# One pass of modulation products ahead of each group's keys, and opening transfers of two feature tiles

## The chip, the cores and the metric

The program runs on one core of a Trainium2 chip. The metric is the device time of one launch in microseconds (us), the median of several runs. The engines of the core are TensorE (PE: matmuls), VectorE (DVE), ScalarE (ACT), GpSimd (POOL) and SyncE (SP), whose part here is to issue transfers; 16 DMA engines move the data. Each engine works through its own queue in order and waits on semaphores.

## The reference, cut to what matters

Two layers of a diffusion backbone over 512 latent tokens and 256 context tokens of 1024 features. What the change touches is how layer 0 begins: a modulation vector is made from the conditioning vector, the inputs are scaled and shifted by it, and the modulated inputs are projected.

```python
silu_c, silu_cc = jax.nn.silu(c), jax.nn.silu(c_ctx)
mod = silu_c @ ada_w[layer] + ada_b[layer]              # 1024 x 6144
sh_m, sc_m, gt_m, sh_f, sc_f, gt_f = split(mod, 6)
u = x * (1 + sc_m) + sh_m                               # 512 x 1024
mod_c = silu_cc @ ada_w[layer][:, :2 * D] + ada_b[layer][:2 * D]
ctx_u = ctx * (1 + mod_c[D:]) + mod_c[:D]               # 256 x 1024
p = u @ w_in                # queries, keys, values, gates, pools, 16 scalars a token
pc = ctx_u @ (the columns of keys, values and scalars of w_in)
...                         # DeltaNet heads || pooling, o = [heads, pools]
y = o @ w_out
x = layernorm(ALPHA * x + gt_m * y)
...                         # ConvFFN, then layer 1
```

## The kernel before

Activations lie with features on the partitions: 8 tiles of 128 features by 512 tokens (latent) and 8 of 128 by 256 (context). An f32 product is made of three passes, high by high, low by high and high by low part: ACT copies the high part out of a tile (`ah`, `ch`, `w_hi`) and DVE or POOL subtracts it from the tile to get the low part (`al`, `cl`, `w_lo`). A projection's matmuls all stand in the helper `gemm` (L222).

The opening is `start` (from L241). The scale and shift columns that layer 0 needs first are 2048 columns of `ada_w`, in 4 groups g of 512: group g holds what the feature tiles 2g and 2g+1 need. One group goes through these steps:

- eight 128x512 f32 tiles `ada_w` (256 KB each) arrive by SP's queue; PE multiplies each by the two conditioning vectors `cs` (L289), the first four and the last four tiles into the same four strips of `ada_ps`;
- ACT copies the sums out as `ada_rows` (L304), PE turns them into columns `ada_t` with small matmuls (L311), and DVE adds the biases: `m` (L320);
- DVE scales and shifts the two tiles `x_in` (each as two halves of 256 tokens) and `c_in` (L325), ACT copies their high parts (L452), DVE and POOL make the low parts (L453);
- PE adds the two tiles' share of the 16 scalars, `scalars(g)` (L342, 8 matmuls into `scal_ps`), and of the first keys, `keys(2g)` and `keys(2g+1)` (L222, 12 matmuls each into `qkv_ps`), whose weights were split earlier.

The order on PE is written out by hand: products of the first four tiles of group g+1, `scalars(g)`, `keys(2g)`, products of the last four tiles of group g+1, `keys(2g+1)`, `ada_t` of group g+1. After the fourth group come `scalars(3)`, `keys(6)`, `keys(7)`, and then the small matmuls `sc_t` (L699), with which the opening ends for what follows here. Instructions that the code pins keep the order of the program; a scheduler places the others.

SP issues the transfers in the order of the program: per group eight `ada_w`, then for each of two feature tiles two halves of `x_in` and one `c_in`; behind the first and the second group two raw weight tiles, and at the end `even_k`, raw weights and `crow`. All these tiles borrow buffers of the pool "even" that later stages use under other names (`BUFS` gives their numbers, `tags` and `htags` the order in which they are borrowed).

One place far behind the opening matters too, the output projection of layer 0 (`out_proj`, in the trace from 330 to 400 us). There the residual tiles `z` are loaded by SP (L1321) into a new pool laid over memory of the closed pool "even", so that the loads wait for the last readers of what stood there; behind them in SP's queue come `ada_w` tiles of layer 1, which DVE multiplies by `crow` and sums (L358, the columns `mod` come from these sums, L367). On DVE the same queue holds the evictions `z<-out_ps` (L520) and some of the weight splits `w_lo` (L176).

## Time and profile before

| what | value |
|---|---|
| median of 3 runs | 1341.77 us (1341.52 to 1342.78) |
| the profiled execution, its own time | 1340.33 us |
| span of the profiled execution | 1338.5 us |
| mean granted clock of TensorE | 0.975 of full speed |
| PE busy | 1271.3 us (95%) |
| DVE, POOL, ACT busy | 907.3, 680.5, 583.9 us |
| bytes moved | 166.59 MB |

The profile is of one execution. Its own time is 1.83 us longer than its span and lies 1.44 us below the median. A matmul's busy time includes its overlap with the next one, so a stretch's length is read from starts, not from sums. Times in the rows below count from the span's start. SPq is SP's queue while it issues transfers; "idle before <- releaser" is how long the engine stood idle and what ended it.

### The profile page before, as it was taken

What the parts mean: (1) busy time and instruction counts of PE and PEld (TensorE: products, weight loads), DVE (VectorE), ACT (ScalarE), POOL (GpSimd) and SP (SyncE); (2) the same over time, 40 slices, a digit from 0 to 9 for tenths busy, and PEclk for the clock granted to TensorE, in tenths of its full rate; (3) what the DMA queues carried; (4) which work ended last, traced back from release to release, by engine and by line L of the source; (5) the groups of instructions that cost most, each with busy time, mean ns of one, the idle gap of its engine ahead of it and who ended that gap; (6) DMA issues with size and microseconds to landing.
All of it is one profiled execution on the core that took longest, in us unless ns stands there. A gap on an engine that the chain in (4) does not pass through costs nothing.

```text
span 1338.5 us, 19585 instructions
## 1 busy us (share of the span) xinstructions
PE 1271.3 (95%) x6690; PEld 1069.2 (80%) x6690; DVE 907.3 (68%) x1865; ACT 583.9 (44%) x1091; POOL 680.5 (51%) x616
## 2 busy tenths in 40 slices
PE   6898899989889999999999999999999999999997
PEld 2587777878688888888888988778988888888886
DVE  3397899999776787788644668956676666661125
ACT  2355414445547433333322576545463334332235
POOL 1336447666445665555444566966143433443453
PEclk8899999999988999999999999999899999999998
DMA  9521221522523555656566432323123323333344
GB/s 302 201 87 46 42 60 53 166 83 87 173 81 105 163 189 190 198 194 196 185 206 195 141 111 87 95 87 107 35 95 99 98 95 96 101 91 96 93 123 126
DMA packets 104948, 166.59 MB, mean 124 GB/s; under 512 B 20944, under 2 KB 29200, under 8 KB 104848
## 3 DMA queue, kind: packets, MB, share of 16 engines
q1 hardware_dynamic: 93888, 164.09, 39.2%
q10 hardware_dynamic: 10960, 1.25, 0.7%
q8 instruction: 53, 0.87, 0.3%
q14 instruction: 47, 0.39, 0.1%
HBM read 162.60 MB, written 2.69 MB: 123 GB/s over the span
## 4 chain that ended last, share of the span: by engine, by line
PE 73%; DVE 11%; POOL 4%; issue 3%; ACT 2%; DMA 2%; SPq 0%; ACTq 0%; POOLq 0%; DVEq 0%
PE prod_ps L222 37%; PE out_ps L222 22%; PE half_ps L222 3%; DVE ada_w L358 2%; POOL w_lo L176 1%; PE qkv_ps L222 1%; POOL conf_far L1221 1%; PE ln_e L413 1%; PE it_ps L987 1%; PE gate_ps L222 1%; PE dd_ps L862 1%; DVE x_t L933 1%; DMA ada_w<-in_ada 1%; POOL cb_t L886 1%; PE ln_w L423 1%
## 5 line engine op out<-in xcount | busy, mean ns | idle before, releaser
L176 POOL TENSOR_TENSOR w_lo<-w_raw,w_hi 128x512 fp32r<-128x512 f32 (+1 forms) x299 | 385.0, 1292 | 449.8 <-ACT w_hi L170 441.5
L170 ACT CAST w_hi<-w_raw 128x512 fp32r<-128x512 f32 (+1 forms) x408 | 246.2, 608 | 454.1 <-PE out_ps L222 149.8
L222 PE MATMUL prod_ps<-uh,w_lo 128*128 128x512 f32 x792 | 308.9, 390 | 2.6 <-POOL w_lo L176 2.6
L222 PE MATMUL prod_ps<-uh,w_hi 128*128 128x512 f32 x792 | 308.7, 390 | 0.6 <-ACT w_hi L170 0.6
L222 PE MATMUL prod_ps<-ul,w_hi 128*128 128x512 f32 x792 | 308.4, 389 | 0.0
L601 DVE SCALAR_TENSOR_TENSOR f_acc<-prod_ps,prm,f_acc 128x441 f32<-128x441 f32 (+2 forms) x320 | 222.4, 695 | 60.1 <-ACT f_acc L590 50.8
L176 DVE TENSOR_TENSOR w_lo<-w_raw,w_hi 128x512 fp32r<-128x512 f32 (+1 forms) x109 | 87.0, 799 | 137.7 <-ACT w_hi L170 135.1
L222 PEld LDWEIGHTS prod_ps<-uh,w_lo 128*128 128x128 f32 x792 | 148.7, 188 | 35.2 <-POOL w_lo L176 4.3
L222 PEld LDWEIGHTS prod_ps<-uh,w_hi 128*128 128x128 f32 x792 | 148.8, 188 | 31.9 <-ACT w_hi L170 1.5
L222 PEld LDWEIGHTS prod_ps<-ul,w_hi 128*128 128x128 f32 x792 | 148.7, 188 | 30.4
L222 PE MATMUL out_ps<-ah,w_lo 128*128 128x256 f32 (+1 forms) x352 | 119.6, 340 | 5.6 <-DVE w_lo L176 5.6
L222 PE MATMUL out_ps<-ah,w_hi 128*128 128x256 f32 (+1 forms) x352 | 120.0, 341 | 4.6 <-ACT w_hi L170 2.9
L222 PE MATMUL out_ps<-al,w_hi 128*128 128x256 f32 (+1 forms) x352 | 120.5, 342 | 0.0
L222 PE MATMUL out_ps<-hl,w_hi 128*128 128x512 f32 (+1 forms) x280 | 98.3, 351 | 0.0
L222 PE MATMUL out_ps<-hh,w_hi 128*128 128x512 f32 (+1 forms) x280 | 98.0, 350 | 0.0
L222 PE MATMUL out_ps<-hh,w_lo 128*128 128x512 f32 (+1 forms) x280 | 98.0, 350 | 0.0
L222 PEld LDWEIGHTS out_ps<-ah,w_lo 128*128 128x128 f32 x352 | 68.4, 194 | 12.8 <-DVE w_lo L176 5.9
L222 PEld LDWEIGHTS out_ps<-ah,w_hi 128*128 128x128 f32 x352 | 68.5, 195 | 12.2 <-ACT w_hi L170 3.4
L358 DVE SCALAR_TENSOR_TENSOR ada_w<-ada_w,crow_ps 128x512 f32<-128x512 f32 x112 | 70.8, 683 | 8.7 <-DMA ada_w<-in_ada 8.7
L222 PEld LDWEIGHTS out_ps<-al,w_hi 128*128 128x128 f32 x352 | 68.5, 195 | 7.7 <-DVE al L453 0.8
L222 PEld LDWEIGHTS out_ps<-hl,w_hi 128*128 128x128 f32 x280 | 52.7, 188 | 7.7
L222 PEld LDWEIGHTS out_ps<-hh,w_lo 128*128 128x128 f32 x280 | 52.6, 188 | 7.7
(362 smaller groups left out, 2323.4 us busy)
## 6 DMA issues: line engine op xcount, KB each, us to landing
ada_w<-in_ada SPq DMA_DIRECT2D x192, 256.0 KB, 4.0
w_raw<-in_ffn_up SPq DMA_DIRECT2D x176, 256.0 KB, 2.6
w_raw<-in_ffn_down SPq DMA_DIRECT2D x100, 256.0 KB, 2.7
w_raw<-in_even_in SPq DMA_DIRECT2D x40, 256.0 KB, 2.9
w_raw<-in_odd_in SPq DMA_DIRECT2D x40, 256.0 KB, 2.7
w_raw<-in_even_out SPq DMA_DIRECT2D x16, 256.0 KB, 2.8
w_raw<-in_odd_out SPq DMA_DIRECT2D x16, 256.0 KB, 2.8
w_raw<-in_ffn_down SPq DMA_DIRECT2D x20, 128.0 KB, 2.1
```

What stands on the lines that cost most here:

```text
L170: r = nc.scalar.copy(out=hi[:, :n], in_=raw)
L176: r = eng.tensor_tensor(out=lo[:, :n], in0=raw, in1=hi[:, :n].bitcast(F32), op=SUB)
L222: r = nc.tensor.matmul(out=o, lhsT=w, rhs=x[k][:, c0:c1], start=clear and k == i == 0, stop=k == n - 1 and i == 2, skip_group_check=pin)
L358: r = nc.vector.scalar_tensor_tensor(out=w, in0=w, scalar=1.0, in1=c, op0=MUL, op1=MUL, accum_out=self.mod[:, k, i:i + 1])
L413: nc.tensor.matmul(out=pe[:, 2 * (n * e + i):2 * (n * e + i) + 2], lhsT=t[:, i * P:(i + 1) * P], rhs=ones, start=e == 0 and i == 0 and not ...
L423: nc.tensor.matmul(out=o, lhsT=self.ones, rhs=d[:, 0:n].rearrange("p a b -> p (a b)"), start=True, stop=True)
L601: nc.vector.scalar_tensor_tensor(out=o, in0=sv[:, r0 + dr:r1 + dr, q0 + dc:q1 + dc], scalar=w[:, tap:tap + 1], in1=o, op0=MUL, op1=ADD)
L862: nc.tensor.matmul(out=o, lhsT=self.tri[:, 2 + d], rhs=r, start=d == 0, stop=d == 1)
L886: nc.gpsimd.tensor_tensor(out=t, in0=m[:, 2 * c:2 * c + 2], in1=self.mask(self.blk, 2), op=MUL)
L933: nc.vector.tensor_tensor(out=t, in0=a2[w, :, r, r + 1:16][:, :, None, :].broadcast_to([96, 2, m, m]), in1=x[w, :, r + 1:16, r + 1:16].rea ...
L987: nc.tensor.matmul(out=pt[:, h], lhsT=m[:, h], rhs=r1[:, h], start=True, stop=True)
L1221: nc.gpsimd.tensor_tensor(out=far, in0=far, in1=f, op=ADD)
```

## The change

In the opening the transfers are made larger: `ada_w` tiles come two at a time (128x1024, 512 KB), `x_in` comes as one 128x1024 transfer for the two feature tiles of a group and `c_in` as one of 128x512. They have buffers of their own in a pool "start", which is closed at the end of the opening: 12 of `ada_w`, 3 (`XB`) each of `x_in` and `c_in`. PE makes the products of all eight tiles of group g+1 in one go, then `scalars(g)`, then `ada_t` of group g+1, and only then `keys(2g)` and `keys(2g+1)`. One more weight, `even_in[6]`, is split at a pinned place in the fourth group; its raw tiles stand at the same place in SP's queue as before. The tiles of `big` and `t2` move to a pool "even2", which is opened when "start" is closed and lies over its memory; the tiles `ch` and `cl` borrow other buffers.

```diff
--- before.py
+++ after.py
@@ -83,10 +83,8 @@
 ODD = 'c0 c1 s0 c2 s1 c3 s2 s3'
 PK, RAWS, SPLITS = 4, 4, 4
 WK = [0, 1]
-EARLY = 1
+XB = 3
 KT = 1
-PIN_ADA = 0
-BIG = ("p0", "p1", "late", "tmp")
 BUFS = dict(p0=4, p1=4, late=4, tmp=5, kc=4, vc=2, vt=5, el=4, ec=2, mg=8, inv=10, z=3, at=2, n1=2, vn=2, kd=4, s0=2, s1=2,
             oo=8, osq=1, ada=4)
 
@@ -241,29 +239,32 @@
     def start(self, km):
 
         nc, a = self.nc, self.a
-        tags = [t for t in ("p0", "p1", "late", "ec", "el", "mg", "vt") for _ in range(self.bufs[t])]
-        htags = [t for t in ("kc", "vc", "n1", "at", "s0", "s1", "kd", "vn", "oo") for _ in range(self.bufs[t])]
+        with ExitStack() as ctx:
+            return self.start_in(km, self.pool("start", ctx=ctx))
+
+    def start_in(self, km, sp):
+        nc, a = self.nc, self.a
+        htags = [t for t in ("n1", "at", "s0", "s1", "kd", "vn", "oo") for _ in range(self.bufs[t])]
         half = lambda i, dt, nm: self.ep.tile([P, C], dt, tag=htags[i], bufs=self.bufs[htags[i]], name=nm)
         aw, xi, ci, wk = [], [], [], {}
+
         for g in range(4):
-            for k in range(KD):
-                t = tags.pop(0) if g < 3 or k < 4 else "ada"
-                w = (self.ada_tile(0) if t == "ada" else self.big("ada_w", t)[:, 0:T] if t in BIG else
-                     self.t2(t, "ada_w").rearrange("p a b -> p (a b)"))
-                nc.sync.dma_start(out=w, in_=a["ada0"][g, :, k])
-                aw.append(w)
-            for k in (2 * g, 2 * g + 1):
-                xi.append([self.ep.tile([P, C], F32, tag="inv", bufs=self.bufs["inv"], name="x_in") for _ in HALVES])
-                for x, (c0, c1) in zip(xi[k], HALVES):
-                    nc.sync.dma_start(out=x, in_=a["xT"][:, k, c0:c1])
-                ci.append(half(k, F32, "c_in"))
-                nc.sync.dma_start(out=ci[k], in_=a["ctxT"][:, k])
+            for k in range(0, KD, 2):
+                w = sp.tile([P, 2, T], F32, tag="aw", bufs=12, name="ada_w")
+                nc.sync.dma_start(out=w, in_=a["ada0"][g, :, k:k + 2])
+                aw += [w[:, 0], w[:, 1]]
+            x = sp.tile([P, 2, T], F32, tag="x", bufs=XB, name="x_in")
+            nc.sync.dma_start(out=x, in_=a["xT"][:, 2 * g:2 * g + 2])
+            xi += [[x[:, i, c0:c1] for c0, c1 in HALVES] for i in range(2)]
+            c = sp.tile([P, 2, C], F32, tag="c", bufs=XB, name="c_in")
+            nc.sync.dma_start(out=c, in_=a["ctxT"][:, 2 * g:2 * g + 2])
+            ci += [c[:, 0], c[:, 1]]
             if g in WK:
                 i = WK.index(g) * PK * P
                 wk[g] = [self.raw(a["even_in"][4 + m][:, i:i + PK * P]) for m in range(2)]
         nc.sync.dma_start(out=km, in_=a["even_k"])
-        self.ch = [half(8 + k, F32R, "ch") for k in range(KD)]
-        self.cl = [half(16 + k, F32R, "cl") for k in range(KD)]
+        self.ch = [half(k, F32R, "ch") for k in range(KD)]
+        self.cl = [half(8 + k, F32R, "cl") for k in range(KD)]
         cs = self.cp.tile([P, KD, 2], F32, name="cs")
         nc.scalar.activation(out=cs, in_=self.cvec, func=AF.Silu)
         raw, wsc = (self.ep.tile([P, C], dt, tag="z", bufs=self.bufs["z"], name=f"scal_{nm}") for nm, dt in
@@ -288,30 +289,31 @@
                 q = 32 * (k % 4)
                 r = nc.tensor.matmul(out=ps[q:q + 2, :], lhsT=cs[:, k, :], rhs=aw[8 * g + k],
                                      start=k < 4, stop=k >= 4, skip_group_check=True)
-                if PIN_ADA:
-                    self.tc.keep_in_program_order(r)
-
-        for g in range(4):
+                self.tc.keep_in_program_order(r)
+
+        def clear():
             ps = self.mm("ada_ps")
             nc.vector.memset(ps, 0.0)
-            ada(g, ps, range(4))
+            return ps
+
+
+        ps = clear()
+        for g in range(4):
+            ada(g, ps, range(KD))
+            rows = sp.tile([P, T], F32, tag="rows", bufs=2, name="ada_rows")
+            nc.scalar.copy(out=rows, in_=ps)
             if g:
                 self.scalars(psc, wsc, g - 1)
-                if EARLY:
-                    keys(2 * g - 2)
-            ada(g, ps, range(4, 8))
-            rows = self.big("ada_rows")[:, 0:T]
-            nc.scalar.copy(out=rows, in_=ps)
-            if g:
-                if not EARLY:
-                    keys(2 * g - 2)
-                keys(2 * g - 1)
             pt = self.gd("ada_t")
             for j in range(4):
                 r = nc.tensor.matmul(out=pt[:, 2 * j:2 * j + 2], lhsT=rows[:, j * P:(j + 1) * P], rhs=self.sel2,
                                      start=True, stop=True)
-                if PIN_ADA:
-                    self.tc.keep_in_program_order(r)
+                self.tc.keep_in_program_order(r)
+            if g < 3:
+                ps = clear()
+            else:
+
+                self.early = {6: [w for x in self.raws(a["even_in"][6]) for w in self.piece(x, pin=True)]}
 
             ptv = pt[:, 0:8].rearrange("p (s n w) -> p s n w", s=2, n=2)
             for s in range(2):
@@ -328,6 +330,9 @@
             if g in wk:
                 for m in range(2):
                     ws[m] += self.piece(wk[g][m], pin=True)
+            if g:
+                keys(2 * g - 2)
+                keys(2 * g - 1)
         self.scalars(psc, wsc, 3)
         keys(6)
         keys(7)
@@ -634,6 +639,7 @@
             self.ep = self.pool("even", ctx=ctx)
             self.ada_tile = lambda k: self.ep.tile([P, T], F32, tag="ada", bufs=self.bufs["ada"], name="ada_w")
             first, scal = self.start(km)
+            self.ep2 = self.pool("even2", ctx=ctx)
             self.dp = ctx.enter_context(self.tc.tile_pool(name="scratch", bufs=1, space=bass.MemoryType.DRAM))
             self.gate = [None] * H
             ps, pooled, self.decays = {}, [], {}
@@ -673,7 +679,7 @@
         self.dbg("mixl", self.al)
 
     def big(self, name, tag="tmp"):
-        return self.ep.tile([P, T + 16], F32, tag=tag, bufs=self.bufs[tag], name=name)
+        return self.ep2.tile([P, T + 16], F32, tag=tag, bufs=self.bufs[tag], name=name)
 
     def t1(self, tag, name=None):
 
@@ -681,7 +687,7 @@
 
     def t2(self, tag, name=None):
 
-        return self.ep.tile([P, 4, P], F32, tag=tag, bufs=self.bufs[tag], name=name or tag)
+        return self.ep2.tile([P, 4, P], F32, tag=tag, bufs=self.bufs[tag], name=name or tag)
 
     def gates(self, scal):
 
@@ -788,7 +794,7 @@
     def qkv(self, m, lat, con, pre=None):
 
         nc, ep = self.nc, self.ep
-        ws = pre or self.weights(self.a["even_in"][m])
+        ws = pre or self.early.pop(m, None) or self.weights(self.a["even_in"][m])
         w = self.gconv[:, m]
         for x, h, l, n in ((con, self.ch, self.cl, C), (lat, self.ah, self.al, T)):
             if x is None:
```

On PE, in the opening: `ada_ps` are the products, `ada_t` the columns' matmuls, `scal_ps` the scalars, `qkv_ps` the keys. Before, the last four products of group 1 stand between the two blocks of keys of group 0:

```order
L222 MATMUL qkv_ps<-cl,w_hi 128x256
L222 MATMUL qkv_ps<-ch,w_lo 128x256
L289 MATMUL ada_ps<-ada_w,cs 2x512 x4
L222 MATMUL qkv_ps<-ah_75,w_hi 128x512
L222 MATMUL qkv_ps<-al_83,w_hi 128x512
```

and the columns of that group stand behind both blocks (the first rows are the end of `keys(1)`):

```order
L222 MATMUL qkv_ps<-cl,w_hi 128x256
L222 MATMUL qkv_ps<-ch,w_lo 128x256
L311 MATMUL ada_t<-prm,ada_rows 128x2 x4
L289 MATMUL ada_ps<-ada_w,cs 2x512 x4
L342 MATMUL scal_ps<-ah_76,scal_w 32x512
L342 MATMUL scal_ps<-al_84,scal_w 32x512
L342 MATMUL scal_ps<-ch,scal_w 32x256
L342 MATMUL scal_ps<-cl,scal_w 32x256
L342 MATMUL scal_ps<-ah_77,scal_w 32x512
```

Now, from the columns of group 0 on:

```order
L309 MATMUL ada_t<-prm,ada_rows 128x2 x4
L290 MATMUL ada_ps<-ada_w,cs 2x512 x8
L347 MATMUL scal_ps<-ah_74,scal_w 32x512
L347 MATMUL scal_ps<-al_82,scal_w 32x512
L347 MATMUL scal_ps<-ch,scal_w 32x256
L347 MATMUL scal_ps<-cl,scal_w 32x256
L347 MATMUL scal_ps<-ah_75,scal_w 32x512
L347 MATMUL scal_ps<-al_83,scal_w 32x512
L347 MATMUL scal_ps<-ch,scal_w 32x256
L347 MATMUL scal_ps<-cl,scal_w 32x256
L309 MATMUL ada_t<-prm,ada_rows 128x2 x4
L220 MATMUL qkv_ps<-ah_74,w_hi 128x512
```

All eight products of group 1 stand ahead of the scalars of group 0, and the columns of group 1 ahead of the keys of group 0.

On SP, in the opening, one group's transfers before, with the start of the next group:

```order
L253 DMA ada_w<-in_ada 128x512 x8
L258 DMA x_in<-in_xT 128x256 x2
L260 DMA c_in<-in_ctxT 128x256
L258 DMA x_in<-in_xT 128x256 x2
L260 DMA c_in<-in_ctxT 128x256
L162 DMA w_raw<-in_even_in 128x512 x2
L253 DMA ada_w<-in_ada 128x512 x8
```

and now:

```order
L254 DMA ada_w<-in_ada 128x1024 x4
L257 DMA x_in<-in_xT 128x1024
L260 DMA c_in<-in_ctxT 128x512
L160 DMA w_raw<-in_even_in 128x512 x2
L254 DMA ada_w<-in_ada 128x1024 x4
```

The group's bytes and their place in the queue are the same; 14 transfers have become 6.

On SP, in the output projection, the eight loads of `z` and the first of `ada_w` with the semaphores that they wait for, before:

```order
L1321 DMA z_3535<-in_xT 128x512 [waits DMAHW5_49,DMAHW0_49,DMAHW6_49,DVE_49,DMAHW7_49,PE_49,Pool_49]
L1321 DMA z_3536<-in_xT 128x512
L1321 DMA z_3537<-in_xT 128x512
L1321 DMA z_3538<-in_xT 128x512
L1321 DMA z_3539<-in_xT 128x512 [waits DMAHW1_49]
L1321 DMA z_3540<-in_xT 128x512 [waits DMAHW2_49]
L1321 DMA z_3541<-in_xT 128x512 [waits DMAHW3_49]
L1321 DMA z_3542<-in_xT 128x512 [waits DMAHW4_49]
L356 DMA ada_w<-in_ada 128x512 [waits DMAHW5_49]
L356 DMA ada_w<-in_ada 128x512 [waits DMAHW6_49]
```

and now:

```order
L1327 DMA z_3479<-in_xT 128x512 [waits DMAHW5_49,DMAHW0_49,DMAHW6_49,DVE_49,DMAHW7_49,PE_49,Activation_49]
L1327 DMA z_3480<-in_xT 128x512
L1327 DMA z_3481<-in_xT 128x512
L1327 DMA z_3482<-in_xT 128x512
L1327 DMA z_3483<-in_xT 128x512 [waits DMAHW1_49]
L1327 DMA z_3484<-in_xT 128x512 [waits DMAHW2_49]
L1327 DMA z_3485<-in_xT 128x512 [waits DMAHW3_49]
L1327 DMA z_3486<-in_xT 128x512 [waits DMAHW4_49]
L361 DMA ada_w<-in_ada 128x512 [waits DMAHW5_49,DVE_49,Pool_49]
L361 DMA ada_w<-in_ada 128x512 [waits DMAHW6_49]
```

The `z` loads no longer wait for POOL; the first `ada_w` behind them now waits for DVE and POOL itself. DVE's value for `z` was that of its last `al<-gate` split, and is now that of `oo<-oo,oss`, six rows of DVE ahead of it.

On DVE, in the output projection, from that last split on, before:

```order
L453 TENSOR_TENSOR al_89<-gate,ah_81 128x512
L176 TENSOR_TENSOR w_lo<-w_raw,w_hi 128x512
L520 SCALAR_TENSOR_TENSOR z_3535<-out_ps,mod_g,z_3535 128x512
L520 SCALAR_TENSOR_TENSOR z_3536<-out_ps,mod_g,z_3536 128x512
L358 SCALAR_TENSOR_TENSOR ada_w,mod<-ada_w,crow 128x512 x4
L520 SCALAR_TENSOR_TENSOR z_3537<-out_ps,mod_g,z_3537 128x512
L358 SCALAR_TENSOR_TENSOR ada_w,mod<-ada_w,crow 128x512 x4
L367 TENSOR_TENSOR mod_3757<-mod 128x16
L368 TENSOR_TENSOR mod_3757<-mod_3757,prm 128x16
L377 SCALAR_TENSOR_TENSOR cols_f_3760<-mod_3757,prm 128x8
L378 SCALAR_TENSOR_TENSOR cols_f_3760<-mod_3757,prm 128x8
L379 TENSOR_TENSOR cols_f_3760<-cols_f_3760,mod_3757 128x8
```

and now:

```order
L458 TENSOR_TENSOR al_89<-gate,ah_81 128x512
L174 TENSOR_TENSOR w_lo<-w_raw,w_hi 128x512
L363 SCALAR_TENSOR_TENSOR ada_w,mod<-ada_w,crow 128x512
L525 SCALAR_TENSOR_TENSOR z_3479<-out_ps,mod_g,z_3479 128x512
L363 SCALAR_TENSOR_TENSOR ada_w,mod<-ada_w,crow 128x512 x3
L525 SCALAR_TENSOR_TENSOR z_3480<-out_ps,mod_g,z_3480 128x512
L363 SCALAR_TENSOR_TENSOR ada_w,mod<-ada_w,crow 128x512 x3
L525 SCALAR_TENSOR_TENSOR z_3481<-out_ps,mod_g,z_3481 128x512
L363 SCALAR_TENSOR_TENSOR ada_w,mod<-ada_w,crow 128x512
L174 TENSOR_TENSOR w_lo<-w_raw,w_hi 128x512
L372 TENSOR_TENSOR mod_3701<-mod 128x16
L373 TENSOR_TENSOR mod_3701<-mod_3701,prm 128x16
```

The sums over `ada_w` stand earlier between the evictions of `z`, and a `w_lo` stands ahead of the columns `mod` instead of behind them.

## Rows read from the trace of the kernel before

**Rows 1.** The page: span, granted clock in 40 slices, chain that ended last.

```profile
span 1338.5 us, 19585 instructions
...
PEclk8899999999988999999999999999899999999998
...
PE 73%; DVE 11%; POOL 4%; issue 3%; ACT 2%; DMA 2%; SPq 0%; ACTq 0%; POOLq 0%; DVEq 0%
```

**Rows 2.** Windows view: stretch, its length, busy us (records) of five engines, PEclk, DMA share, GB/s.

```profile
4.00:42.00 38.00, 29.37 (x144) 13.62 (x144) 11.78 (x38) 10.47 (x24) 8.41 (x9) 0.91 1.00 328
7.50:12.50 5.00, 5.00 (x16) 0.61 (x14) 0.00 (x0) 0.00 (x0) 0.00 (x0) 1.00 1.05 367
15.00:22.00 7.00, 4.09 (x10) 0.60 (x11) 4.71 (x11) 3.22 (x8) 3.95 (x4) 0.51 0.99 338
...
45.80:49.20 3.40, 3.40 (x12) 2.82 (x11) 0.00 (x0) 0.00 (x0) 0.00 (x0) 0.50 1.01 383
...
56.00:62.80 6.80, 5.95 (x18) 4.00 (x19) 2.47 (x6) 3.01 (x7) 3.89 (x5) 0.50 0.14 41
47.50:50.00 2.50, 2.50 (x15) 1.74 (x15) 0.00 (x0) 0.00 (x0) 0.00 (x0) 0.66 1.02 397
```

**Rows 3.** Timeline of PE, the opening: start us, us, instruction [idle before it <- releaser].

```profile
17.91 3.73 PE L289 MATMUL ada_ps<-ada_w,cs 128*2 128x512 f32 x8 [3.28 <-DMA ada_w<-in_ada]
21.57 0.54 PE L342 MATMUL scal_ps<-ah,scal_w 128*32 128x512 f32 x1
...
23.11 0.40 PE L222 MATMUL qkv_ps<-ah,w_hi 128*128 128x512 f32 x1
...
49.56 1.04 PE L289 MATMUL ada_ps<-ada_w,cs 128*2 128x512 f32 x8
50.53 0.50 PE L222 MATMUL qkv_ps<-ah,w_hi 128*128 128x512 f32 x1
...
52.73 0.95 PE L311 MATMUL ada_t<-prm,ada_rows 128*128 128x2 f32 x8
...
57.88 0.64 PE L342 MATMUL scal_ps<-ah,scal_w 128*32 128x512 f32 x1 [0.39 <-ACT ah L452]
...
59.26 0.63 PE L222 MATMUL qkv_ps<-ah,w_hi 128*128 128x512 f32 x1
...
65.17 1.51 PE L699 MATMUL sc_t<-even_k,sc_rows 32*128 32x16 f32 x12
```

**Rows 4.** Timeline of DVE, the opening: the fourth group's columns.

```profile
53.72 0.23 DVE L320 SCALAR_TENSOR_TENSOR m<-ada_t,prm 128x4 f32<-128x4 f32 x2 [8.18 <-PE ada_t L311]
```

**Rows 5.** Timeline of SP: issue of the fourth group's eight ada_w transfers.

```profile
32.44 3.94 SPq L253 DMA_DIRECT2D ada_w<-in_ada  x8
```

**Rows 6.** Tile view of ada_w, the first 52 us: its last line.

```profile
DMA to landing us min/median/max: 3.5/5.8/6.5
```

**Rows 7.** Waits of SP from 335 to 420 us: total us, times, longest.

```profile
SPq L1321 <- DVE al L453: 9.6, 1, 9.6
```

**Rows 8.** Timeline of SP from 340 us: the z loads.

```profile
349.10 3.65 SPq L1321 DMA_DIRECT2D z<-in_xT  x8
```

**Rows 9.** Timeline of DVE, output projection of the first layer.

```profile
342.45 0.41 DVE L1139 TENSOR_TENSOR oo<-oo,oss 128x256 f32<-128x256 f32 x1
...
353.07 0.75 DVE L520 SCALAR_TENSOR_TENSOR z<-out_ps,mod_g,z 128x512 f32<-128x512 f32 x1 [3.50 <-ACT z L1322]
...
359.39 0.99 DVE L358 SCALAR_TENSOR_TENSOR ada_w<-ada_w,crow 128x512 f32<-128x512 f32 x1 [2.85 <-DMA ada_w<-in_ada]
...
370.73 1.11 DVE L367 TENSOR_TENSOR mod<-mod 128x16 f32<-128x16 f32 x1
...
372.44 0.69 DVE L176 TENSOR_TENSOR w_lo<-w_raw,w_hi 128x512 fp32r<-128x512 f32 x1
...
377.72 0.48 DVE L520 SCALAR_TENSOR_TENSOR z<-out_ps,mod_g,z 128x256 f32<-128x256 f32 x1 [3.33 <-PE out_ps L222]
```

**Rows 10.** Timeline of PE, the same place.

```profile
373.19 0.58 PE L222 MATMUL out_ps<-ah,w_lo 128*128 128x256 f32 x1 [5.62 <-DVE w_lo L176]
```


## The prediction

> **What bounds the kernel now.** I read the page first. PE is the end of most of the chain (73%), with DMA at 2% and engines that feed PE for the rest [rows 1], so a change that leaves PE's work alone can only win where PE waits. The clock line names the places: full level nearly everywhere, the lowest digit in the first slice [rows 1]. So I went to the opening, and there to the stretches. From 4 to 42 us the DMA engines are busy all the time (share 1.00) and move 328 GB/s, while PE's records add up to 29 of 38 us [rows 2]: the stream of inputs sets the pace. PE's timeline shows it: the products of group 1 from 17.91 begin after 3.28 us of waiting for `ada_w` [rows 3].
>
> But the end of the opening isn't set by the stream alone. SP issues the fourth group's `ada_w` from 32.44 to 36.38 [rows 5], and such a tile lands 5.8 us after its issue at the median and 6.5 at most [rows 6]: all weights of the modulation are there by 42.2. PE makes their last products only at 49.56, behind `scalars(2)` and `keys(4)`, makes the columns at 52.73 behind `keys(5)` as well [rows 3], and DVE, which stood idle for 8.18 us, gets its columns at 53.72 [rows 4]. From there to `sc_t` at 65.17 nothing of the stream is missing. So about 11.5 us lie between the last landing and the columns, in which PE did work that could have waited. Part of that is the clock: granted 0.50 (1.2 GHz) from 45.8 to 49.2, where 12 matmuls of `keys(4)` take 3.40 us, and again 0.50 from 56.0 to 62.8 [rows 2]; `keys(5)` at the full level took 52.73 - 50.53 = 2.2 us [rows 3].
>
> A second place, far behind, came out of the order of SP and DVE. In the output projection SP waits 9.6 us for a split on DVE [rows 7], issues the `z` loads at 349.10 (for 3.65 us) [rows 8] and the `ada_w` tiles behind them; DVE waits for the first of these until 359.39 and sums until 370.73; a `w_lo` stands behind that at 372.44 [rows 9], and PE waits 5.62 us for it, until 373.19 [rows 10].
>
> **The change, part by part.** No multiplication is added or removed. *Larger transfers* (14 issues of a group become 6): the bytes are the same, and the stream has no gap to fill. The bounds: 47.5 to 50.0, with 4 KB rows in it (`crow`), moved 397 GB/s, and the best stretch of 2 KB rows, 7.5 to 12.5, moved 367 [rows 2], which is 8% of 38 us = 2.9 us; at the other end, a pair is usable only when both halves are there, nothing gained. I take the middle, 1.5 us, and set the last landing at 42.2 - 1.5 = 40.7. The queue is never empty, so fewer issues on SP are worth nothing by themselves.
>
> *The new order on PE*, from that landing:
> - eight products, 1.04 us [rows 3]: 41.7;
> - `scalars(2)`, 23.11 - 21.57 = 1.54 us [rows 3]: 43.3. Its data are there: a group's stream takes 38 / 4 = 9.5 us, so group 2's ends at 31.2, its columns are made at 34.8 and its data modulated at 39. ACT copies `ada_rows` under the scalars;
> - `ada_t` to columns, 53.72 - 52.73 = 1.0 us [rows 3, 4]: columns at 44.3, PE free at 44.2;
> - PE does `keys(4)` and `keys(5)`, 2 x 2.2: 48.6. Beside it the fourth group is modulated: 57.88 - 53.72 = 4.2 us to the last `ah` that the scalars want [rows 3, 4], 48.5, so it is just hidden;
> - `scalars(3)` 1.54, `keys(6)` and `keys(7)` 4.4: 54.6, and `sc_t` begins there instead of at 65.17: **-10.6 us**.
>
> PE is idle before 40.7: with the same terms from 31.2 on, `keys(2)` and `keys(3)` are done at 39.1, 1.6 us before they would be late. The fourth group's `x_in` and `c_in`, 786 KB behind its `ada_w`, take 2.4 us at 328 GB/s and land at 43.1, ahead of the columns. The new waits: `ada(g+1)` stands at the head of PE's queue, and `scalars(g)` and both `keys` queue behind it; they cost nothing as long as they fit between two landings. The fourth `x_in` waits in SP's queue for group 0's buffer, with `ada_w` of no later group behind it; those were read before `keys(0)` began at 23.11 [rows 3], and SP comes there behind the issue that ended at 36.38. The pinned split of `even_in[6]` adds one copy ahead of the second `sc_rows` on ACT, with 4.4 us of keys as cover; without that cover it costs one copy, under a microsecond. What follows `sc_t` hangs on PE, DVE and weight buffers that PE frees, all of which move with it, so I carry the 10.6 through.
>
> *The second place.* With the tiles of `big` and `t2` in another pool, `z` waits for `oo<-oo,oss`, done at 342.86 [rows 9], so its loads can go 349.10 - 342.86 = 6.2 us earlier. The `ada_w` behind them still wait for the split that released `z` before, and can be issued at 349.1; with the shortest landing of such a tile, 3.5 [rows 6], that is 352.6, so the 6.2 stand: the first at 359.39 - 6.2 = 353.2. From there 370.73 - 359.39 = 11.3 for the eight sums [rows 9], and two evictions of 0.75 which lay in the wait [rows 9], now among the sums: 366.0; `w_lo` comes directly behind (the small `mod` operations that took 372.44 - 370.73 = 1.7 now come later) and takes 0.69 [rows 9]: PE goes on at 366.7 instead of 373.19, up to -6.5. But behind it DVE's next wait for PE is only 3.33 us (until 377.72) [rows 9]: beyond that DVE binds again. Bounds 0 and -6.5; I take the 3.3, since that row is the nearest limit: **-3.3 us**.
>
> Sum: -13.9. The profiled execution took 1340.33 us (span 1338.5 [rows 1] and 1.83 around it), 1.44 below the median of 1341.77; it becomes 1326.4, the median **1327.9**.
>
> **The rivals.**
> *The second place gives nothing* (R1): DVE now meets the sums before the evictions of `z`; where a sum waits for its tile, the evictions wait behind it, and PE may lack a bank. Then -10.6: 1331.2.
>
> *The clock takes part of it back* (R2). The rows show 0.51 from 15 to 22, after PE had waited for transfers, and 0.50 twice more [rows 2]. In the new order PE waits for a landing once a group, with everything behind it. If PE then works at 1.2 GHz, 12 matmuls take 3.4 instead of 2.2, a factor of 1.55: from 41.7, `scalars(2)` 2.4, `ada_t` 0.9, `keys(4)` and `keys(5)` 6.8, `scalars(3)` 1.54, 4.4 more: 57.8, -7.4 and -10.7 with the second place: 1331.1. The Trainium skill (TensorE: Matmul & The Clock Gate, HAM oscillation) tells that a kernel whose bursts of matmuls are shorter than the waits for transfers between them starts each burst at the lower clock; the stretch at 15 agrees, and 22 to 45 runs at full level here, so that the trace bears the rule out in part only.
>
> *The stream gains more* (R3): at 367 instead of 328 GB/s over 38 us the landing comes 4.0 earlier, 2.5 more than I took; 1325.4. The Trainium skill (DMA: Bandwidth & Descriptors, Measured) gives 0.95 us for 64 KB and 6.15 us for 1 MB and asks for batches of 1 MiB; my estimate from its two figures is 2.0 us for 256 KB and 3.4 us for 512 KB, 15% less for the same bytes, 5.7 us of 38; by the page the sum would be 4.2 lower than mine. The trace shows no such gap between transfers, since several are in flight and the share is 1.00 [rows 2].
>
> *Slower* (R4): pairs land late and PE's tail is cold. From the landing to `sc_t` PE has 13.9 us of work in my sum; at the factor 1.55 it is 21.5, and 65.17 is met again if the last pair lands at 43.7. From there on each microsecond of landing is one of loss; at 300 instead of 328 GB/s it would be 42.2 + 3.5 = 45.7, +2.0, with nothing at the second place: 1343.8. Against it: no stretch of large rows was slow, and the lower level lasted 7 us at most.
>
> *The opening isn't on the path* (R5): a later wait, for weights or on DVE, swallows the shift, and the time is within 0.2% of before. Against it: transfers behind the opening wait for `w_lo` buffers, and those for PE.
>
> **How the numbers follow.** Chances: forecast 0.48 (1327.9, of itself 1323.5 to 1332.5), R1 0.17, R2 0.16, R3 0.09, R5 0.06, R4 0.04. R1 with R2 together is 1334.4. The range of 1322 to 1334.5 leaves out R4, R5 and the outer parts of the others. A measurement tells about 0.2%, 2.7 us, from no change: faster 0.90, same 0.06, slower 0.04.
>
> **What would show it.** Right: products of eight in one go, columns of group 3 near 44.3, `sc_t` near 54.6; SP's issue of `z` near 343 minus the shift of the opening, PE's wait for `w_lo` there gone or short. Wrong: landing of the last pair after 42 (stream term), granted clock of 0.5 between 41 and 55 (R2), a wait of PE for `scalars(3)`'s `ah` above 1 us (modulation not hidden), evictions of `z` late and PE waiting for a bank (R1), or a start of the next stage that moved less than `sc_t` did (R5).

## The result, and the profile after

The changed kernel takes 1326.87 us (median of 4 runs, 1325.18 to 1328.17) against 1341.64 us for the kernel before beside it; the ratio is 0.9888 with a 95% interval of 0.9872 to 0.9905: 1.1% faster. The profiled execution took 1327.21 us, 13.1 less than the profiled one of before.

The page of the changed kernel: span, granted clock in 40 slices, chain that ended last (before: [rows 1]).

```profile
span 1325.4 us, 19571 instructions
...
PEclk9998899999899999999999999989999999999998
...
PE 65%; POOL 4%; DVE 2%; ACT 2%; issue 2%; DMA 2%; SPq 0%; POOLq 0%; ACTq 0%; DVEq 0%
```

DVE's share of that chain fell from 11% to 2%. The windows view of the changed kernel (stretch, its length, busy us and records of PE, weight loads, DVE, ACT and POOL, granted clock, DMA share, GB/s), the answer to [rows 2]:

```profile
14.00:37.00 23.00, 20.37 (x116) 11.92 (x117) 12.89 (x34) 9.67 (x23) 9.53 (x10) 0.93 1.03 408
24.20:51.80 27.60, 27.60 (x178) 20.57 (x176) 14.47 (x38) 11.91 (x29) 10.13 (x12) 1.00 0.76 292
```

and of the kernel before for the first of these stretches:

```profile
14.00:37.00 23.00, 18.59 (x94) 9.56 (x97) 10.02 (x26) 7.04 (x17) 7.95 (x8) 0.85 0.99 320
```

The stream moves 408 instead of 320 GB/s at the same DMA share of about 1, and from 24.2 to 51.8 PE is busy for all of the 27.6 us at the full level. PE's timeline in the opening (start, us, instruction), the answer to [rows 3]:

```profile
29.41 1.90 PE L290 MATMUL ada_ps<-ada_w,cs 128*2 128x512 f32 x16
...
37.82 1.90 PE L290 MATMUL ada_ps<-ada_w,cs 128*2 128x512 f32 x16
39.65 0.42 PE L347 MATMUL scal_ps<-ah,scal_w 128*32 128x512 f32 x1
...
41.07 0.95 PE L309 MATMUL ada_t<-prm,ada_rows 128*128 128x2 f32 x8
41.88 0.48 PE L220 MATMUL qkv_ps<-ah,w_hi 128*128 128x512 f32 x1
...
46.14 0.40 PE L347 MATMUL scal_ps<-ah,scal_w 128*32 128x512 f32 x1
...
47.55 0.40 PE L220 MATMUL qkv_ps<-ah,w_hi 128*128 128x512 f32 x1
...
51.83 1.40 PE L705 MATMUL sc_t<-even_k,sc_rows 32*128 32x16 f32 x11
```

The products of groups 2 and 3 now come in one piece each (a product shows as two records), at 29.41 and 37.82, and `sc_t` starts at 51.83 instead of 65.17. DVE's columns of the fourth group, which were at 53.72 [rows 4]:

```profile
42.06 0.23 DVE L322 SCALAR_TENSOR_TENSOR m<-ada_t,prm 128x4 f32<-128x4 f32 x2 [3.67 <-PE ada_t L309]
```

The tile view of `ada_w` in the opening, last line, the answer to [rows 6]; by the records of the single transfers the last pair was issued at 27.16 and landed at 36.70, where the last tile landed at 42.33 before:

```profile
DMA to landing us min/median/max: 7.3/8.4/9.5
```

At the second place, SP's timeline (before: [rows 8]), then DVE's and PE's (before: [rows 9, 10]):

```profile
331.12 3.88 SPq L1327 DMA_DIRECT2D z<-in_xT  x8
336.48 7.25 SPq L361 DMA_DIRECT2D ada_w<-in_ada  x7
```

```profile
329.89 0.41 DVE L1145 TENSOR_TENSOR oo<-oo,oss 128x256 f32<-128x256 f32 x1
...
342.68 0.69 DVE L363 SCALAR_TENSOR_TENSOR ada_w<-ada_w,crow 128x512 f32<-128x512 f32 x1 [5.66 <-DMA ada_w<-in_ada]
...
352.57 1.75 DVE L174 TENSOR_TENSOR w_lo<-w_raw,w_hi 128x512 fp32r<-128x512 f32 x1
354.25 1.24 DVE L372 TENSOR_TENSOR mod<-mod 128x16 f32<-128x16 f32 x1
...
374.68 0.16 DVE L444 COPY ln_q<-ln_e 128x2 f32<-128x2 f32 x1 [4.17 <-PE ln_e L418]
```

```profile
354.38 0.58 PE L220 MATMUL out_ps<-ah,w_lo 128*128 128x256 f32 x1 [2.86 <-DVE w_lo L174]
...
369.66 1.13 PE L418 MATMUL ln_e<-onesn,ln_s 128*128 128x2 f32 x8 [1.21 <-DVE ln_s L402]
```

Everything up to here starts 12.56 us earlier than before (`oo<-oo,oss` at 329.89 against 342.45). Beyond that, the `z` loads go 5.4 us earlier, the first sum over `ada_w` 4.2 and PE's restart behind `w_lo` 6.3 (354.38 against 373.19, less 12.56).

Where the time went along the run, read from timelines: start of the same instruction against the kernel before, in us of the profiled executions.

| place, with its time before | changed | e1 memory | e2 order | e4 short rows | e6 single ada_w | e8 weights behind |
|---|---|---|---|---|---|---|
| `sc_t`, 65.2 | -13.3 | -0.5 | -10.2 | -13.0 | -13.2 | -14.2 |
| first `oo`, 256.8 | -13.3 | 0.0 | -7.9 | -13.3 | -13.3 | -12.5 |
| `oo` that frees `z`, 342.5 | -12.6 | +0.7 | -7.8 | -12.6 | -13.2 | -11.9 |
| layer norm's columns `ln_q`, 389.4 | -14.7 | -2.3 | -10.5 | -16.0 | -16.8 | -14.7 |
| next layer norm, 759.5 | -15.5 | -0.5 | -8.0 | -13.2 | -13.1 | -13.3 |
| end of the span, 1338.5 | -13.1 | +0.3 | -9.0 | -17.1 | -10.2 | -13.8 |

### The profile page after: what moved, and what is told of

Same layout as the page of the kernel before. It is cut to its first block, busy times and chain, and to the rows that moved or that the text cites. A ratio compares the mean times of both kernels' runs of the same rounds, so it can differ in the third digit from the quotient of the medians.

```text
span 1325.4 us, 19571 instructions
## 1 busy us (share of the span) xinstructions
PE 1266.8 (96%) x6690; PEld 1068.8 (81%) x6690; DVE 910.5 (69%) x1865; ACT 584.8 (44%) x1091; POOL 679.1 (51%) x616
## 4 chain that ended last, share of the span: by engine, by line
PE 65%; POOL 4%; DVE 2%; ACT 2%; issue 2%; DMA 2%; SPq 0%; POOLq 0%; ACTq 0%; DVEq 0%
PE prod_ps L220 37%; PE out_ps L220 21%; PE half_ps L220 3%; POOL w_lo L174 1%; PE ln_e L418 1%; POOL conf_far L1227 1%; PE ln_w L428 1%; DMA z<-in_xT 0%; PE gate_ps L220 0%; ACT w_hi L168 0%; DVE ln_s L405 0%; DMA w_raw<-in_odd_out 0%; POOL ln_s L402 0%; DVE ln_d L425 0%; DVE z L479 0%
```

## The experiments

Theory A: the new order lets PE use what has landed and is most of the gain; larger transfers make the stream faster and add the rest; the second place comes from the memory. Its rivals are named with the runs. All times against the kernel before on the same chip.

**e1, the memory alone** (with the pinned split of `even_in[6]`, which all these kernels have). Transfers of before (diff against the changed kernel) and, as in e3 below, the order of before:

```diff
-                w = sp.tile([P, 2, T], F32, tag="aw", bufs=12, name="ada_w")
-                nc.sync.dma_start(out=w, in_=a["ada0"][g, :, k:k + 2])
+                w = sp.tile([P, T], F32, tag="aw", bufs=24, name="ada_w")
+                nc.sync.dma_start(out=w, in_=a["ada0"][g, :, k])
...
-            x = sp.tile([P, 2, T], F32, tag="x", bufs=XB, name="x_in")
-            nc.sync.dma_start(out=x, in_=a["xT"][:, 2 * g:2 * g + 2])
+                for x, (c0, c1) in zip(xi[k], HALVES):
+                    nc.sync.dma_start(out=x, in_=a["xT"][:, k, c0:c1])
...
```

> Only the memory changes: the tiles of the opening have buffers in the pool start, big and t2 lie in even2, the split of even_in[6] is pinned as after; transfers (8 tiles of 256 KB, x halves, single c) and the order on PE are those of before. Theory A (larger transfers make the stream faster, the order lets PE use it, the second place comes from the memory alone): the stream at about 328 GB/s from 4 to 42 us, last columns near 53.7, sc_t near 65.2, the z loads 5 to 6 us earlier against the split they waited for, and 2 us less in all (1339 to 1340). Rival B (the place of the buffers made the stream fast): about 400 GB/s here already, sc_t at 60 or earlier, total 1333 or less.

Measured: 0.9988 of before (0.9977 to 0.9999), median 1339.24. The stream:

```profile
14.00:37.00 23.00, 18.41 (x98) 9.50 (x97) 10.03 (x26) 7.04 (x17) 7.99 (x8) 0.93 1.00 336
```

336 GB/s against 320 before, and `sc_t` at 64.66: the place of the buffers did little for the stream, so rival B falls. The gain of 1.6 us is at the edge of what can be told.

**e2, memory and order, transfers of before** (the transfers of e1 in the changed kernel).

> As the changed kernel, but with the transfers of before (single ada_w tiles, x halves, single c), so the memory and the order on PE. Theory A: the stream stays at about 328 GB/s, the last ada_w lands near 42.2, and with 13.9 us of PE behind it sc_t starts near 56 (9 us earlier than before, 4.3 later than with larger transfers); total 1330 to 1331. Rival C (order is everything, the transfers nothing): sc_t near 52, total 1327.

Measured: 0.9933 (0.9918 to 0.9948), median 1331.79.

```profile
14.00:37.00 23.00, 19.52 (x96) 9.35 (x96) 10.17 (x29) 7.68 (x19) 7.99 (x8) 0.93 0.97 317
```

```profile
55.02 1.51 PE L705 MATMUL sc_t<-even_k,sc_rows 32*128 32x16 f32 x12
```

With the slow stream the order, together with the memory (0.5 in e1), brings 10.2 of the 13.3 us; rival C falls, since `sc_t` is 3.2 us later than with the large transfers. Two things change with the order, the products in one piece and the columns ahead of the keys; no run has one without the other.

**e3, memory and transfers, order of before:**

```diff
-            ada(g, ps, range(KD))
+            ada(g, ps, range(4))
+            if g:
+                self.scalars(psc, wsc, g - 1)
+                keys(2 * g - 2)
+            ada(g, ps, range(4, 8))
...
             if g:
-                self.scalars(psc, wsc, g - 1)
+                keys(2 * g - 1)
```

> As the changed kernel, but with the order on PE of before, so the memory and the larger transfers. Theory A: the stream at about 400 GB/s, but columns follow each other by PE's loop of 11.3 us (columns, 4.2 of modulation, scalars 1.5, keys 2.2, half of the products 0.5, keys 2.2, ada_t 1.0), so last columns near 50, sc_t near 59.5; total 1333 to 1334. Rival D (the transfers are everything): sc_t near 52, total 1327. If the clock falls to the lower level in the opening as before, 3 us more.

Measured: 1.0139 (1.012 to 1.0158), slower. The stream, and PE at the end of the opening:

```profile
14.00:37.00 23.00, 18.70 (x101) 10.24 (x102) 10.15 (x26) 7.26 (x19) 8.01 (x8) 0.93 1.03 408
```

```profile
64.86 1.51 PE L706 MATMUL sc_t<-even_k,sc_rows 32*128 32x16 f32 x12
```

A stream as fast as in the changed kernel, with the last pair landed at 36.3, and `sc_t` 0.3 us earlier than before and 0.2 later than in e1: under the old order the stream isn't what the opening ends on, and rival D falls. I had expected 59.5; columns followed each other by 13.4, 11.3 and 13.5 us instead of 11.3, the last with the granted clock at 0.50 from 42.4 to 49.0. This kernel's median is 18.6 us above that of before, and that arises behind the opening (its first gate product, at 154.2 before, is 11.3 us late): the scheduler puts instructions that aren't pinned into another order there (SP has 26 weight tiles in a row where the changed kernel has two rows of `ada_w` between). So only the opening of e3 answers the question, and its total says nothing of the transfers.

**What makes the stream fast** took six more kernels. In e4 the instructions are those of the changed kernel, with a gap in each SBUF tile, so that the pieces are half as long:

```diff
-                w = sp.tile([P, 2, T], F32, tag="aw", bufs=12, name="ada_w")
+                w = sp.tile([P, 2, T + 16], F32, tag="aw", bufs=12, name="ada_w")[:, :, 0:T]
```

> The changed kernel with the same instructions, but a gap of 64 bytes between the two halves of each ada_w, x_in and c_in tile in SBUF, so that a transfer is as large as after and its contiguous pieces are half as long (2 KB, c_in 1 KB). Theory A1 (the length of the pieces makes the rate): back to about 330 GB/s, with packets that take far longer than the usual 84 ns, sc_t near 56, total 1330 to 1331. Theory A2 (the number of transfers makes it): 390 GB/s or more, sc_t near 52, total as after, 1327.

Measured: 0.9889 (0.9869 to 0.9909), median 1324.91, as the changed kernel.

```profile
14.00:37.00 23.00, 20.10 (x114) 11.72 (x115) 12.58 (x34) 9.61 (x23) 9.23 (x10) 0.93 1.06 384
```

384 GB/s: pieces of half the length cost 6% of the rate, not 22%. So it is rather the transfers' size or number, A2. e5 and e6 tell which of the transfers, e5 with `x_in` and `c_in` in the transfers of before, e6 with `ada_w` in those of before.

> The changed kernel with x_in as halves of 256 tokens and c_in one tile at a time, as before (12 small transfers a pair of groups more, pieces of 1 KB), ada_w still in pairs. If the small transfers of x_in and c_in slowed the stream: about 340 GB/s from 14 to 37 us, the last ada_w near 41, sc_t near 55. If it was the single ada_w tiles: 390 GB/s or more, last ada_w near 37 to 38, sc_t near 52.

> The changed kernel with ada_w one tile of 256 KB at a time, as before, x_in and c_in still as pairs. If the single ada_w tiles slowed the stream: about 340 GB/s from 14 to 37 us, last ada_w near 41, sc_t near 55. If it was x_in and c_in: 390 GB/s or more, sc_t near 52. If both come out near 370 GB/s, the number of transfers as such counts and each has a part.

Measured, one run each: 1335.74 and 1330.10 (before on that chip: 1339.62). First e5, then e6:

```profile
14.00:37.00 23.00, 19.49 (x101) 9.39 (x100) 9.91 (x28) 8.22 (x19) 8.02 (x8) 0.85 0.96 323
```

```profile
14.00:37.00 23.00, 20.84 (x114) 11.80 (x114) 12.70 (x34) 9.16 (x22) 9.34 (x10) 0.85 1.05 391
```

The edits are the lines of e1's diff for `x_in` in e5 and for `ada_w` in e6. The 256 KB tiles of `ada_w` are nearly as good as pairs (391 GB/s, `sc_t` at 52.0); it is the six small transfers a group of `x_in` and `c_in`, where the changed kernel has two, that make the stream slow (323, `sc_t` at 55.6). e9 and e10 were to part the length of their pieces from their size. In e9 `x_in` comes as two transfers of 256 KB with pieces of 1 KB, in e10 as four of 128 KB with pieces of 2 KB:

```diff
+            x = [sp.tile([P, 2, C], F32, tag="x", bufs=2 * XB, name="x_in") for _ in HALVES]   # e9
+            for t, (c0, c1) in zip(x, HALVES):
+                nc.sync.dma_start(out=t, in_=a["xT"][:, 2 * g:2 * g + 2, c0:c1])
...
+                for p0 in (0, 64):                                                             # e10
+                    nc.sync.dma_start(out=x[p0:p0 + 64], in_=a["xT"][p0:p0 + 64, 2 * g + i])
```

> The changed kernel with x_in in two transfers of 256 KB, one per half of the tokens, each for both tiles, and c_in with a gap between its tiles: all pieces of x_in and c_in are 1 KB as before, but no transfer is smaller than 256 KB and there is one more a group than in the changed kernel. If the 1 KB pieces slowed the stream: about 325 to 340 GB/s from 14 to 37 us, sc_t near 55. If it was the size of the transfers (128 KB), which land in quick succession and let SP issue in bursts: 385 GB/s or more, sc_t near 52.

> The changed kernel with x_in and c_in in transfers of 128 KB that cover 64 partitions each: six a group as before, but pieces of 2 KB. If small transfers in succession slow the stream: about 325 to 340 GB/s from 14 to 37 us, sc_t near 55. If it was the 1 KB pieces: 385 GB/s or more, sc_t near 52. (A transfer of 64 partitions may use the DMA engines unevenly, which would slow the stream too; then the stretch of x_in itself is slow, not the ada_w behind it.)

In e11 the small transfers of before stand between the pairs:

```diff
                 aw += [w[:, 0], w[:, 1]]
+                j = 2 * g + k // 4
+                if k % 4 == 0:
...
+                    for x, (c0, c1) in zip(xi[j], HALVES):
+                        nc.sync.dma_start(out=x, in_=a["xT"][:, j, c0:c1])
```

> The changed kernel with x_in and c_in in the transfers of before (halves of 128 KB, c_in of 128 KB, pieces of 1 KB), but spread in SP's queue between the ada_w pairs of their group instead of standing behind them. If a run of small transfers, which empties the queue's bytes and lets SP issue in a burst, slows the stream: spread out they cost little, 380 GB/s or more from 14 to 37 us, though the last ada_w of a group lands up to 1.9 us later than in the changed kernel because its x_in and c_in now come ahead of it: sc_t 52 to 54. If each small transfer or each 1 KB piece costs by itself: 325 to 340 GB/s, last ada_w at 43 or later, sc_t at 56 or later.

Measured, one run each: e9 1325.46, e10 1334.64, e11 1345.48 (before on that chip: 1342.03, one run). In this order e9, e10 and e11:

```profile
14.00:37.00 23.00, 20.31 (x114) 11.39 (x113) 12.13 (x34) 9.75 (x23) 8.88 (x10) 0.85 1.05 391
```

```profile
14.00:37.00 23.00, 19.37 (x104) 9.43 (x103) 9.65 (x28) 8.22 (x19) 7.96 (x8) 0.85 0.98 325
```

```profile
14.00:37.00 23.00, 20.54 (x108) 9.84 (x107) 10.30 (x29) 8.40 (x20) 8.04 (x8) 0.85 1.01 371
```

Short pieces in transfers of 256 KB cost little (391), and the small transfers of before cost less than half as much when they don't stand in a run (371 against 323, with 408 without them). So it is their size, and more than half of it their standing in a run. e11 lies between the two outcomes that were expected: its last `ada_w` landed at 41.12, and `sc_t` came at 55.1, hardly earlier than in e5; a group's small transfers now land ahead of its last pair.

e10 (325) settles nothing about the pieces, for what its expectation feared came about. By the records of the transfers the six small ones of its third group land in 3.76 us (33.26 to 37.02), where those of e5 take 2.07 (33.09 to 35.16), and the first pair of that group lands 1.3 us behind the transfer ahead of it, so there the stretch of `x_in` and `c_in` is slow itself. SP's timeline shows what goes with a run of small transfers, e5 first and then e6:

```profile
22.80 1.84 SPq L254 DMA_DIRECT2D ada_w<-in_ada  x4
24.68 1.60 SPq L259 DMA_DIRECT2D x_in<-in_xT  x2
26.33 0.67 SPq L261 DMA_DIRECT2D c_in<-in_ctxT  x1
27.04 2.53 SPq L259 DMA_DIRECT2D x_in<-in_xT  x2
```

```profile
22.70 2.38 SPq L254 DMA_DIRECT2D ada_w<-in_ada  x4
25.41 0.33 SPq L257 DMA_DIRECT2D x_in<-in_xT  x1
26.09 0.33 SPq L260 DMA_DIRECT2D c_in<-in_ctxT  x1
26.84 5.02 SPq L254 DMA_DIRECT2D ada_w<-in_ada  x7
```

In e5 the small ones land quickly and SP issues eight transfers back to back from 22.8 to 27.5, some taking up to 1.1 us instead of 0.33; the pair issued at 22.80 lands 3.4 us behind the transfer ahead of it, where a pair takes 1.3 in an undisturbed stretch. In e6 SP issues one each 0.67 us. Whether the emptied queue or the burst of issues slows the engines isn't parted here. e11's total suffers from another order behind the opening, as e3's does.

**e7, the `z` loads late again**, by one small copy on DVE:

```diff
+        nc.vector.tensor_copy(out=self.zs[0][:, 0:1], in_=self.al[7][:, 0:1].bitcast(F32))
```

> The changed kernel with one small copy on DVE behind its last split in the output projection, from which the first z load must wait: the z loads start where they did before (5.3 us later than in the changed kernel, near 336.5), all else as there. If the second place is worth what the profiles show up to the layer norm (2.2 us): the layer norm's columns 2 to 4 us later, total 1329 to 1331. Rival: what is won there is given back by TensorE's lower level behind it, as in the kernel with the memory alone: total within 1 us of the changed kernel.

Measured: 0.9906 (0.9873 to 0.994), median 1329.0, 2.1 above the changed kernel, which their ranges (1325.53 to 1330.22 and 1325.18 to 1328.17) can't tell apart. And the edit did only half of what it should:

```profile
330.74 7.33 SPq L1328 DMA_DIRECT2D z<-in_xT  x8
```

```profile
336.14 0.15 DVE L1326 COPY z<-al 128x1 f32<-128x1 f32 x1
...
342.78 0.69 DVE L363 SCALAR_TENSOR_TENSOR ada_w<-ada_w,crow 128x512 f32<-128x512 f32 x1 [5.82 <-DMA ada_w<-in_ada]
```

Four of the eight `z` went at 330.7 and only the others waited for the copy at 336.14, so the first sum over `ada_w` is 0.1 us later than in the changed kernel, and the layer norm's columns are 1.1 later, where 2 to 4 were expected. The run doesn't price the second place; e1 does, as far as it can be.

**e8, two weights' transfers behind the `ada_w` of groups 1 and 3:**

```diff
-            if g in WK:
-                i = WK.index(g) * PK * P
+            if g in (1, 3):
+                i = g // 2 * PK * P
                 wk[g] = [self.raw(a["even_in"][4 + m][:, i:i + PK * P]) for m in range(2)]
```

(these lines now stand ahead of the group's `x_in`, and the splits behind the copy of `ada_rows`).

> The changed kernel with the two key weights' transfers (512 KB each) moved behind the ada_w of groups 1 and 3, and split behind the copies of ada_rows of these groups. At 405 GB/s 512 KB are 1.3 us, so ada_w of groups 1 to 3 land 1.3 us earlier; PE is busy without a gap from the scalars of group 0 on, so sc_t near 50.6 instead of 51.83, and the total 1.2 us less if nothing behind changes. If PE's chain isn't bound by the landing of group 1's ada_w, sc_t stays at 51.8.

Measured: 0.9884 (0.9856 to 0.9913), median 1325.14; `sc_t` at 50.94, 0.9 earlier than in the changed kernel, but only 0.3 earlier than in e7 (51.28), whose opening is that of the changed kernel. So the step can't be told from the scatter of the profiles, nor in the total.

## Why the prediction was right, point by point

The forecast was 1327.9 (-13.9), measured 1326.87; in the profiled executions -13.1. It was right in sum and sign, but the sum is nearer than its terms, and that is luck: the opening gave 2.7 us more than forecast and the second place 1.1 less, and 0.8 between the places and 1.6 behind them were given back, which no term had.

*What bounds.* Right: under the old order the opening ends on PE's own loop. e3 shows it: a stream 88 GB/s faster than before moved `sc_t` by 0.3 us.

*The new order.* The tail from the last landing was put at 13.9 us; from the start of the last products (37.82) to `sc_t` (51.83) it took 14.0, and from the landing (36.70) 15.1. That the work fits is partly luck: I took 1.04 us for eight products from a row with x8, but a product has two records and that row was four of them; eight take 1.83 (37.82 to 39.65). The scalars (1.42 instead of 1.54), `ada_t` (0.81 instead of 0.95) and each pair of keys (4.3 instead of 4.4) made it up. With the transfers of before (e2) `sc_t` came at 55.0; the sum with no gain of the stream gives 42.2 + 13.9 = 56.1. The last tile landed at 41.84 there, and PE had begun the products at 40.40, while tiles still came.

*The stream.* This term was mis-sized: 1.5 us, measured 5.6 (landing at 36.70 instead of 42.33). The step that failed is the upper bound of 2.9 us: it set 397 GB/s against the best stretch, 367, and not against the 328 that the stream moved. Against 328 the same rows give 38 x (1 - 328 / 397) = 6.6 us and 38 x (1 - 328 / 367) = 4.0, the figure of R3, which already lay above my bound. And the stretch with 367 still held the cause, `x_in` and `c_in` in small transfers. The estimate from the Trainium skill (DMA: Bandwidth & Descriptors, Measured), 5.7 us, was nearer, though the page's rows are of transfers that GpSimd issues and these are SP's. But its figures make the size of every transfer count, those of `ada_w` above all, and e6 shows that single tiles of 256 KB do as well within 4% while the runs of 128 KB do the harm. From e2 to the changed kernel the last landing moved by 5.1 us (41.84 to 36.70) and `sc_t` by only 3.2: PE has no gap left from 24.2 on, so a landing 1.1 us ahead of its products brings nothing more. So R3 came about: `sc_t` is 2.8 us ahead of the forecast 54.6, 1.7 of it from the stream and 1.1 from the order (e2).

*The clock in the opening* (R2) didn't fall: 1.00 from 24.2 to 51.8, where before had two stretches at 0.50. e2 has 1.00 from 24.2 to 55.0 as well, e1 and e3 have 0.87 from 24 to `sc_t`, so the level follows the order and not the transfers, and part of the order's gain is the clock. The price in R2 was too low: six matmuls of `keys` took 1.92 us at the lower level (59.26 [rows 3] to 61.18) and 1.04 at the full one (34.60 to 35.64 in the changed kernel), a factor of 1.85 and not 1.55. The 12 records in the window from which I took 3.40 are two of the scalars and ten of `keys(4)`; its twelve took 3.71 (45.85 to 49.56), the last two at the full level. With 1.85 my estimate for the 3.40 and 5.95 us that PE worked at the lower level in the two stretches of [rows 2] is 9.35 x (1 - 1 / 1.85) = 4.3 us, of the 13.3. The rows of before, and the two of the changed kernel for the six matmuls:

```profile
45.85 0.63 PE L222 MATMUL qkv_ps<-ah,w_hi 128*128 128x512 f32 x1
...
61.18 0.63 PE L222 MATMUL qkv_ps<-ah,w_hi 128*128 128x512 f32 x1
```

```profile
34.60 0.39 PE L220 MATMUL qkv_ps<-ah,w_hi 128*128 128x512 f32 x1
...
35.64 0.39 PE L220 MATMUL qkv_ps<-ah,w_hi 128*128 128x512 f32 x1
```

*Between the places* 0.8 us were given back (-13.3 to -12.6 in the table), which no term had; e1 and e4 lose 0.7 there too. The cause stays open.

*The second place.* PE's restart was forecast 6.5 us earlier and is 6.3, by errors that cancel. The first `ada_w` took 6.2 us from its issue to its sum (336.48 to 342.68) and not the 3.5 of the shortest landing, so that the sum came 4.2 us earlier and not 6.2; the sums and the evictions among them took 9.9 us (to 352.57) and not 12.8; the `w_lo` took 1.75 and not 0.69. R1 didn't come about: no wait for a bank shows on PE ahead of 354.38.

The columns of the layer norm were forecast 3.3 earlier and are 2.2. The reason I gave for the cut holds: DVE binds again. But its size, taken from a wait of 3.33 us, left out that DVE's own work would grow. From the restart to those columns PE does the same 123 matmuls. Before, the changed kernel and e4:

```profile
373.19:389.39 16.20, 16.20 (x123) 16.20 (x124) 8.78 (x13) 5.72 (x11) 10.02 (x7) 0.89 0.52 163
```

```profile
354.38:374.68 20.30, 19.09 (x123) 18.89 (x124) 14.32 (x19) 5.82 (x11) 13.31 (x10) 0.77 0.42 130
```

```profile
353.42:373.38 19.96, 16.72 (x123) 16.10 (x124) 14.04 (x18) 5.72 (x11) 13.22 (x10) 0.93 0.43 133
```

The stretch takes about 4 us longer in both. In the changed kernel its granted clock is 0.77 instead of 0.89, but that isn't what makes it longer: e4 has 0.93 and takes nearly as long, and so do e1 and e8, with 0.91 and 0.92 (20.3 us each). DVE has 14.0 to 14.4 us of work there instead of 8.78, and PE ends up waiting for it, in e4 for 2.52 us, in the changed kernel, where PE itself is slower, for 1.21 (at 369.66 above):

```profile
368.63 1.11 PE L418 MATMUL ln_e<-onesn,ln_s 128*128 128x2 f32 x8 [2.52 <-DVE ln_s L402]
```

Of DVE's longer work 3.2 us are the five small operations of the columns `mod`, which took 4.9 us (354.25 to the `w_lo` at 359.12) where they took 1.7 before (370.73 to 372.44 [rows 9]). From `oo` to the layer norm's columns the place gives 2.2 us in the changed kernel, 3.0 in e1, 3.4 in e4, 3.6 in e6 and 1.9 in e5, so that the forecast 3.3 lies within the range of these profiles. In e1 alone the next layer norm keeps 1.2 of the 3.0, and the ratio just excludes no gain.

*Behind it* the spans of kernels with the same instructions drift apart: e4 ends 4.0 us ahead of the changed kernel though it is 0.3 behind at `sc_t`, with a mean granted clock of 0.984 against 0.978. Their medians (1324.91 and 1326.87) can't be told apart. So what comes behind the layer norm, 1.6 us given back in the changed kernel, isn't explained here.

## What to carry to other kernels

In a stage fed by a stream, look at what the consumer does between the last landing and its use: here reordering the consumer was worth three times as much as a stream that is a quarter faster, and the faster stream was worth nothing measurable without it. Gather small transfers that stand in a run before enlarging those that are large already. A wait that is taken away gives back only what the next limit leaves: at the second place PE restarted 6.3 us earlier, and the columns behind it came 2.2 earlier, since DVE had over 5 us more to do in between. And when a bound is taken from the best stretch of a record, set it against the mean of the record, not against another good stretch.

## What the runs showed of the hardware that I had not expected

- A run of six transfers of 128 KB slows the larger transfers behind it: 317 to 336 GB/s (before, e1, e2, e5) against 384 to 408 without them (changed, e3, e4, e6, e9) and 371 when they are spread (e11), at a DMA share of 0.96 to 1.06 in all cases. The share doesn't tell a slow stream from a fast one; the GB/s do.
- Halving the contiguous pieces costs 408 to 384 GB/s (e4), two transfers for one of `ada_w` 408 to 391 (e6), by one profile each.
- Small DVE operations can take many times their usual length beside work of POOL: `mod` (128x16) and those after it took 1.24, 1.20, 1.20, 0.15 and 1.13 us from 354.25 on, all while POOL worked; of the five before, the first took 1.11 (370.73 [rows 9]) beside POOL and the other four 0.16 to 0.18, after POOL had stopped at 371.81. POOL before, then in the changed kernel:

```profile
368.43 3.38 POOL L176 TENSOR_TENSOR w_lo<-w_raw,w_hi 128x512 fp32r<-128x512 f32 x2
373.94 1.59 POOL L397 TENSOR_TENSOR ln_s<-ln_s,z 128x512 f32<-128x512 f32 x1 [2.13 <-DVE z L520]
```

```profile
353.73 1.72 POOL L405 TENSOR_TENSOR ln_s<-ln_s,ln_sq 128x512 f32<-128x512 f32 x1
355.41 3.76 POOL L174 TENSOR_TENSOR w_lo<-w_raw,w_hi 128x512 fp32r<-128x512 f32 x3
```

  No run moved POOL's work alone, so that it is the cause isn't shown; one of the five stayed short beside it.
